# A hybrid decoder layer: 189 of TensorE's 128x128 transposes replaced by VectorE block transposes and on-chip transfers of 32x32 blocks

## Chip, cores and metric

The kernel runs on one core of a Trainium2 chip. The metric is device time in microseconds, the median of several executions; one more execution is taken with the hardware profiler, and its trace is what the views below read. Engines are called as in the profile: PE is TensorE's matmul side, PEld its weight loads, DVE is VectorE, ACT ScalarE, POOL GpSimd, SP SyncE, whose queue issues nearly all transfers.

## What is computed

One layer: a mixing part and a gated MLP, with RMSNorms. The mixing part, which the change touches, has an HGRN2 head group (4 heads) and a sliding-window attention group with sinks (8 query heads, 2 key heads). Cut to what matters:

```python
u = rmsnorm(x, norm_mix_w)                      # x: 2048 tokens x 1024
hq, hf, hi, hg, att = split(u @ w_in)
f = lb + (1 - lb) * sigmoid(hf);  k = 1 - f;  v = hi;  q = hq * 128 ** -0.5
# HGRN2: S_t = diag(f_t) S_{t-1} + k_t v_t^T,  o_t = S_t^T q_t   (4 heads of 128)
o_hg = rmsnorm(o, hg_norm_w) * silu(hg)
# attention: each block of 128 queries sees its own and the previous block of 128 keys
scores = q_att @ k_att.T / 8, masked to 0 <= distance < 128
p = exp(scores - m);  p = p / (sum(p) + exp(sink - m))
o_att = p @ v_att
h = x + concat(o_hg, o_att) @ w_out             # then the MLP with a causal convolution
```

The window is one block wide, so in a (query block, previous key block) pair exactly the keys above the diagonal are seen, and in the (query block, own key block) pair those on and below it. Scores of both fit in one 128x128 square: own key where key <= query, previous key elsewhere. The kernel keeps them so.

## The kernel before

Tokens are worked in two halves of 1024 (`NH` = 2, eight blocks of 128 in each). For each half come a mixing stage (tile pool `mix0`, `mix1`) and a feed-forward stage (`ffn0`, `ffn1`). Activations lie with features on partitions and tokens along the row; a "unit" is one projection to 128 features for 1024 tokens: 48 matmuls of 128x512, since each f32 operand is split in a high and a low part (`unit`, L218).

In the mixing stage:

- `att_keys` builds keys `KS` and values `V` (token-major, from four-to-a-bank transposes). The last block of keys and values of half 0 is kept in `kcarry` and `vcarry` (SBUF) for half 1.
- `attend(j)` is a generator for a pair of query heads j and j+4 (j = 0 to 3). Stage `qa` is the query unit. Stage `sc` makes, for each half-group g of 4 blocks, scores (L399), the maximum, exponentials (L421) and scaled probabilities `sc` (L426). Stages `pv` and `pw` (g = 0 and 1) transpose the probabilities with TensorE, four to a bank (`ppt`, L435), multiply them by two masks into `po` (own block) and `pp` (previous block) on DVE (L438), and multiply with `V` (`poT`, L446): own probabilities with the block's own values, previous ones with the previous block's.
- `hgrn(h)` is a generator for head h. Stages `f` and `q` are units; stage `l` builds the scores within a block over seven levels (L517 to L552) and leaves decayed keys `K`; stage `s` transposes `K` to `Kn` (`pkn`, L564, copied by ACT, L565) and forms the states `SS` (L571, L578); stage `p` forms the outputs (L590, L592), normalises them into `on` (L600), transposes them (`pot`, L605) and writes them to `hg` (L607 on ACT or L609 on DVE).
- `project_v` (`v0`, `v1`) are the values of two heads, `g` the gate units, `w` a gate's weights ahead of time, `m` the split of a finished output for the output projection.

The order of the stages is written out by hand in `ORDER`. It gives priorities: a planner then simulates all engines by its own costs and sets each engine's instruction order, so matmuls of a later unit stand in between those of an earlier stage. On the chip each engine and each queue keeps that order and waits by semaphores. Tiles of one `tag` share its `bufs` places: `sc` has 2, `pp` 4, `t4` (`ST`, `Kn`, `on`) 2, `SS` 1; weights have three places for raw data and two for their split parts. PSUM has four banks for units (`mm`) and two each for `hg` and `at`. `out_proj` follows with the mixed heads in the order 0, 4, 1, 5, 2, 6, 7, 3, so pair 3 and head 3 come last.

Of the kernel before, what the change touches and what calls it, by code (L numbers as in the profile page):

```python
# [17 lines left out]
P = 128  # L18
# [3 lines left out]
HALF = 1024  # L22
# [17 lines left out]
ORDER = ("f0 q0 l0 qa0 v0 s0 f1 p0 sc0 w0 pv0 q1 l1 qa1 pw0 g0 s1 qa2 sc1 w1 m4 f2 pv1 g1 p1 m1 q2 pw1 l2 "  # L40
         "sc2 v1 m0 pv2 qa3 s2 p2 pw2 f3 m6 q3 l3 m5 sc3 g2 pv3 pw3 m2 g3 s3 p3").split()
# [8 lines left out]
def hymba_layer(ctx: ExitStack, tc: tile.TileContext, a: dict, out: bass.AP, rows_out: bass.AP):  # L50
# [29 lines left out]
    ones = cp.tile([P, P], F32, name="ones")  # L80
    nc.vector.memset(ones, 1.0)
# [3 lines left out]
    nc.scalar.activation(warm, ones[:, 0:1], AF.Tanh)  # L85
# [5 lines left out]
    kc = cp.tile([P, 2, P], F32R, name="kcarry")  # L91
    vc = cp.tile([P, P], F32, name="vcarry")
# [6 lines left out]
    def constants():  # L99
# [3 lines left out]
        C.prevT = cp.tile([P, P], F32, name="prevT")  # L103
        for t, op, sgn in ((C.own, ALU.is_ge, 1), (C.ownT, ALU.is_ge, -1), (C.prevT, ALU.is_gt, 1)):
            nc.gpsimd.memset(t, 1.0)
            nc.gpsimd.affine_select(out=t, in_=t, compare_op=op, fill=0.0, base=0,
                                    pattern=[[-sgn, P]], channel_multiplier=sgn)
# [226 lines left out]

    def rows(kv):
        return slice(kv * HD, (kv + 1) * HD)

    def att_keys(hf, kv, invb, p):
# [6 lines left out]
        if hf:  # L345
            nc.vector.tensor_copy(KS[:, :, 0:P], kc)
            nc.vector.tensor_copy(V[:, 0], vc)
# [10 lines left out]
        for b in range(NB):  # L358
# [4 lines left out]
            nc.scalar.copy(V[:, 1 + 4 * b:5 + 4 * b].rearrange("p a b -> p (a b)"), pv)  # L363
        if hf + 1 < NH:
            nc.vector.tensor_copy(kc, KS[:, :, HALF:HALF + P])
            nc.vector.tensor_copy(vc, V[:, TT])
        return KS, V

    def attend(hf, j, X, invb, KS, V, mix, p):
# [9 lines left out]
        for g in range(NB):  # L379
# [46 lines left out]
            nc.vector.tensor_tensor(sc, sc, den.unsqueeze(3).to_broadcast([P, 2, 4, P]), op=ALU.mult)  # L426
            scs.append(sc)
        yield
        for g, sc in enumerate(scs):
            pm = []  # L430
            for kv in range(2):
                pm.append([p.tile([P, 4, P], F32, tag="pp", name=n, bufs=4) for n in ("po", "pp")])
                pt = ps("at", "ppt")
                for i in range(4):
                    nc.tensor.transpose(pt[:, i * P:(i + 1) * P], sc[:, kv, i], ident)  # L435
                ptv = pt.rearrange("p (i q) -> p i q", i=4)
                for dst, mk in zip(pm[kv], (C.ownT, C.prevT)):
# [764 lines left out]
```

## Time and profile before

| | |
|---|---|
| median of 3 runs | 2150.38 us (2150.18 to 2150.38) |
| the profiled execution: span, first to last instruction | 2149.0 us; no time beside the span is given, and the median stands 1.4 us above it |
| instructions | 29228 |
| PE busy | 2130.8 us (99%), 11271 matmuls |
| PEld busy | 1790.6 us (83%) |
| DVE busy | 1632.2 us (76%) |
| ACT busy | 1020.2 us (47%) |
| chain that ended last | PE 93%, DVE 5%, ACT 1% |
| DMA | 91147 packets, 254.41 MB, mean 118 GB/s |

A busy PE means that some matmul was under way: matmuls are pipelined, so the sum of their durations is more than the time they hold up what follows. A line of the groups view gives line, engine, operation, tile out<-in, shapes, count, then busy us and mean ns of one, then idle time of the engine just before and what ended it. A line of the timeline gives start and length in us, and "x8" means eight merged neighbours. The windows view is read in two stretches, 94 to 365 us for most of half 0's mixing and 1159 to 1441 us for that of half 1.

### The profile page before, as it was taken

How to read it: one execution, taken by the hardware profiler on the slowest of the kernel's cores; microseconds unless marked ns; L12 is line 12 of the kernel's file. 1: busy time of each engine (PE TensorE's matmuls, PEld its weight loads, DVE VectorE, ACT ScalarE, POOL GpSimd, SP SyncE). 2: the span in 40 equal slices, each digit the busy share in tenths (PEclk: the TensorE clock that was granted, in tenths of full speed). 3: DMA queues.
4: the chain of work that ended last, by engine and by line, in shares of the span. 5: the costliest groups of instructions: out<-in, count | busy, mean ns of one | idle time of the engine just before them, and what ended most of it. 6: DMA issues, size and time to landing. Idle time of an engine off the chain costs nothing.

```text
span 2149.0 us, 29228 instructions
## 1 busy us (share of the span) xinstructions
PE 2130.8 (99%) x11271; PEld 1790.6 (83%) x11271; DVE 1632.2 (76%) x2443; ACT 1020.2 (47%) x1818; POOL 16.2 (1%) x45
## 2 busy tenths in 40 slices
PE   8999999999999999999999999999999999999998
PEld 6988988888888888888889889888888888888887
DVE  6576768788887888785775767677988888787765
ACT  5445554564444445345634446535544444443453
POOL 2000000000000000000000000000000000000000
PEclk9999999999999999999999999999999999999999
DMA  4111012413332334974641111124223323359743
GB/s 158 40 30 40 31 30 79 137 62 125 94 122 89 103 118 147 371 255 145 217 138 40 30 31 33 40 75 158 69 104 103 118 84 122 95 187 398 236 147 133
DMA packets 91147, 254.41 MB, mean 118 GB/s; under 512 B 11136, under 2 KB 13952, under 8 KB 91008
## 3 DMA queue, kind: packets, MB, share of 16 engines
q1 hardware_dynamic: 90576, 252.29, 35.3%
q8 instruction: 88, 1.44, 0.3%
q14 instruction: 51, 0.42, 0.1%
q10 hardware_dynamic: 432, 0.27, 0.0%
HBM read 195.37 MB, written 57.15 MB: 118 GB/s over the span
## 4 chain that ended last, share of the span: by engine, by line
PE 93%; DVE 5%; ACT 1%; issue 1%; DMA 0%; SPq 0%; DVEq 0%; ACTq 0%
PE X L767 7%; PE X L766 7%; PE X L765 7%; PE pop L218 6%; PE q L218 4%; PE f L218 4%; PE hq L218 4%; PE Y L767 4%; PE Y L765 4%; PE Y L766 4%; PE pdx L954 3%; PE pdx L953 3%; PE pdx L952 3%; PE g L218 3%; PE pdy L953 3%; PE pdy L954 3%
## 5 line engine op out<-in xcount | busy, mean ns | idle before, releaser
L638 ACT CAST whi<-raw 128x1024 fp32r<-128x1024 f32 x88 | 92.7, 1053 | 115.5 <-PE X L766 71.1
L765 PE MATMUL X<-T,whi 128*128 128x512 f32 x352 | 136.9, 389 | 0.0
L766 PE MATMUL X<-T,whi 128*128 128x512 f32 x352 | 136.9, 389 | 0.0
L767 PE MATMUL X<-T,wlo 128*128 128x512 f32 x352 | 136.9, 389 | 0.0
L836 DVE SCALAR_TENSOR_TENSOR y<-ga,cw,y 128x1024 f32<-128x1024 f32 x88 | 112.7, 1280 | 25.9 <-ACT y L834 25.8
L639 DVE TENSOR_TENSOR wlo<-raw,whi 128x1024 fp32r<-128x1024 f32 x88 | 107.3, 1219 | 4.4 <-ACT whi L638 4.4
L771 ACT COPY u<-X 128x512 f32<-128x512 f32 x88 | 51.6, 586 | 122.5 <-PE X L767 122.2
L199 ACT CAST whi<-raw 128x1024 fp32r<-128x1024 f32 x58 | 60.5, 1048 | 98.8 <-issue 20.6
L639 DVE TENSOR_TENSOR xld<-raw,xhd 128x1024 fp32r<-128x1024 f32 x72 | 81.1, 1132 | 17.8 <-ACT xhd L638 17.6
L638 ACT CAST xhd<-raw 128x1024 fp32r<-128x1024 f32 x72 | 69.8, 978 | 39.1 <-DMA raw<-act0T 14.0
L218 PE MATMUL pop<-XL,whi 128*128 128x512 f32 x256 | 84.2, 392 | 0.9 <-DVE XL L230 0.9
L218 PE MATMUL pop<-XH,wlo 128*128 128x512 f32 x256 | 83.3, 391 | 0.8 <-DVE wlo L200 0.8
L218 PE MATMUL pop<-XH,whi 128*128 128x512 f32 x256 | 83.1, 396 | 0.8 <-ACT XH L229 0.5
L200 DVE TENSOR_TENSOR wlo<-raw,whi 128x1024 fp32r<-128x1024 f32 x58 | 70.5, 1220 | 9.8 <-ACT whi L199 9.8
L767 PEld LDWEIGHTS X<-T,wlo 128*128 128x128 f32 x352 | 66.1, 188 | 13.7
L766 PEld LDWEIGHTS X<-T,whi 128*128 128x128 f32 x352 | 66.1, 188 | 13.7
L765 PEld LDWEIGHTS X<-T,whi 128*128 128x128 f32 x352 | 66.0, 188 | 13.7
L630 PE MATMUL pvv<-whi,XH 128*128 128x256 f32 x256 | 73.0, 286 | 0.0
L631 PE MATMUL pvv<-whi,XL 128*128 128x256 f32 x256 | 72.9, 286 | 0.0
L632 PE MATMUL pvv<-wlo,XH 128*128 128x256 f32 x256 | 71.9, 285 | 0.0
L767 PE MATMUL X<-B,wlo 128*128 128x512 f32 x176 | 68.7, 390 | 0.7 <-DVE wlo L639 0.7
L765 PE MATMUL X<-T,Sh 128*128 128x512 f32 x176 | 68.7, 390 | 0.0
(390 smaller groups left out, 6399.2 us busy)
## 6 DMA issues: line engine op xcount, KB each, us to landing
wr<-in_w_down SPq DMA_DIRECT2D x90, 512.0 KB, 5.6
raw<-in_w_gate SPq DMA_DIRECT2D x44, 512.0 KB, 3.6
raw<-in_w_up SPq DMA_DIRECT2D x44, 512.0 KB, 3.6
raw<-act0T SPq DMA_DIRECT2D x20, 512.0 KB, 5.9
raw<-act1T SPq DMA_DIRECT2D x20, 512.0 KB, 5.6
act0B<-y SPq DMA_DIRECT2D x33, 256.0 KB, 2.3
act1B<-y SPq DMA_DIRECT2D x33, 256.0 KB, 2.4
raw<-in_w_out SPq DMA_DIRECT2D x16, 512.0 KB, 3.7
```

Source lines behind the costliest of these rows:

```text
L218: nc.tensor.matmul(o[b], w, x[:, bs], start=f, stop=l)
L630: nc.tensor.matmul(o[:, 0:256], xh[:, t], hi[:, c], start=kt == 0, stop=False)
L631: nc.tensor.matmul(o[:, 0:256], xl[:, t], hi[:, c], start=False, stop=False)
L632: nc.tensor.matmul(o[:, 0:256], xh[:, t], lo[:, c], start=False, stop=kt == KT - 1)
L638: nc.scalar.copy(h, src)
L639: return (eng or nc.vector).tensor_tensor(l, src, h.bitcast(F32), op=ALU.subtract)
L765: nc.tensor.matmul(o, wh[:, ws], xh, start=i == 0 and not more, stop=False, skip_group_check=more)
L766: nc.tensor.matmul(o, wh[:, ws], xl, start=False, stop=False, skip_group_check=more)
L767: nc.tensor.matmul(o, wl[:, ws], xh, start=False, stop=i == 3, skip_group_check=more)
L836: nc.vector.scalar_tensor_tensor(y, g[:, w:w + HALF], C.cw[:, ft, w:w + 1], y, op0=ALU.mult, op1=ALU.add)
L953: nc.tensor.matmul(o, wh[:, i, c], al[:, i, cols], start=False, stop=False, skip_group_check=more)
L954: nc.tensor.matmul(o, wl[:, i, c], ah[:, i, cols], start=False, stop=l, skip_group_check=more)
```

## The change

- Probabilities of pairs 0 to 2: DVE transposes each of the sixteen 32x32 blocks of a 128x128 square in place (`turned`), and 16 transfers on SP's queue put the blocks in their new places (`moved`). Pair 3 still goes through TensorE, and ACT then copies its transposed probabilities out of PSUM.
- Keys `Kn` and head outputs of heads 0 to 2: the same. Head 3 still goes through TensorE. The keys are turned at the end of stage `l`; the head outputs at the end of stage `p`, and what reads them is a new stage `x`.
- Values: `VD` is each block's values less the previous block's. Whole transposed probabilities times the previous values, plus own (masked) probabilities times `VD`, replaces the two masked products. The mask `prevT` goes; each probability tile is masked once in place of twice.
- The carried keys and values lie in DRAM and move by transfers. `ones` goes.
- `ORDER`: `q1` stands ahead of `pv0`, `q2` ahead of `m1`, and the four `x` stages are added. The last state is copied out earlier.

```diff
@@ -37,8 +37,8 @@
 UP_AFTER = 'T2'
-ORDER = ("f0 q0 l0 qa0 v0 s0 f1 p0 sc0 w0 pv0 q1 l1 qa1 pw0 g0 s1 qa2 sc1 w1 m4 f2 pv1 g1 p1 m1 q2 pw1 l2 "
-         "sc2 v1 m0 pv2 qa3 s2 p2 pw2 f3 m6 q3 l3 m5 sc3 g2 pv3 pw3 m2 g3 s3 p3").split()
+ORDER = ("f0 q0 l0 qa0 v0 s0 f1 p0 sc0 w0 q1 pv0 x0 l1 qa1 pw0 g0 s1 qa2 sc1 w1 m4 f2 pv1 g1 p1 q2 x1 m1 pw1 l2 "
+         "sc2 v1 m0 pv2 qa3 s2 p2 pw2 f3 m6 q3 x2 l3 m5 sc3 g2 pv3 pw3 m2 g3 s3 p3 x3").split()
 LEVELS = [1, 2, 4, 8, 16, 32, 64]
@@ -77,19 +77,18 @@
     nc.scalar.dma_start(nmw, a["norm_mix_w"])
-    ones = cp.tile([P, P], F32, name="ones")
-    nc.vector.memset(ones, 1.0)
     ident = cp.tile([P, P], F32, name="ident")
     warm = cp.tile([P, 32], F32, name="warm")[:, 0:1]
-    nc.scalar.activation(warm, ones[:, 0:1], AF.Tanh)
+    nc.vector.memset(warm, 1.0)
+    nc.scalar.activation(warm, warm, AF.Tanh)
     nc.gpsimd.memset(ident, 1.0)
     nc.vector.memset(halo, 0.0)
-    kc = cp.tile([P, 2, P], F32R, name="kcarry")
-    vc = cp.tile([P, P], F32, name="vcarry")
+    kc = dp.tile([P, 2, P], F32, name="kcarry")
+    vc = dp.tile([P, P], F32, name="vcarry")
@@ -100,8 +99,7 @@
         C.ownT = cp.tile([P, P], F32, name="ownT")
-        C.prevT = cp.tile([P, P], F32, name="prevT")
-        for t, op, sgn in ((C.own, ALU.is_ge, 1), (C.ownT, ALU.is_ge, -1), (C.prevT, ALU.is_gt, 1)):
+        for t, op, sgn in ((C.own, ALU.is_ge, 1), (C.ownT, ALU.is_ge, -1)):
             nc.gpsimd.memset(t, 1.0)
@@ -332,6 +330,17 @@
+    def moved(dst, src):
+
+        for a in range(4):
+            for c in range(4):
+                nc.sync.dma_start(dst[32 * c:32 * c + 32, :, 32 * a:32 * a + 32],
+                                  src[32 * a:32 * a + 32, :, 32 * c:32 * c + 32])
+
+    def turned(dst, src):
+
+        nc.vector.transpose(dst.rearrange("p a b -> p (a b)"), src.rearrange("p a b -> p (a b)"))
+
     def rows(kv):
@@ -343,8 +352,8 @@
         if hf:
-            nc.vector.tensor_copy(KS[:, :, 0:P], kc)
-            nc.vector.tensor_copy(V[:, 0], vc)
+            nc.sync.dma_start(KS.bitcast(F32)[:, :, 0:P], kc)
+            nc.sync.dma_start(V[:, 0], vc)
         kT, vT = [p.tile([P, HALF], F32, tag="f", name=n, bufs=2) for n in ("kT", "vT")]
@@ -361,12 +370,18 @@
             nc.scalar.copy(V[:, 1 + 4 * b:5 + 4 * b].rearrange("p a b -> p (a b)"), pv)
+        VD = p.tile([P, TT, P], F32, name="VD")
+        if hf:
+            nc.vector.tensor_tensor(VD, V[:, 1:], V[:, 0:TT], op=ALU.subtract)
+        else:
+            nc.scalar.copy(VD[:, 0], V[:, 1])
+            nc.vector.tensor_tensor(VD[:, 1:], V[:, 2:], V[:, 1:TT], op=ALU.subtract)
         if hf + 1 < NH:
-            nc.vector.tensor_copy(kc, KS[:, :, HALF:HALF + P])
-            nc.vector.tensor_copy(vc, V[:, TT])
-        return KS, V
-
-    def attend(hf, j, X, invb, KS, V, mix, p):
+            nc.sync.dma_start(kc, KS.bitcast(F32)[:, :, HALF:HALF + P])
+            nc.sync.dma_start(vc, V[:, TT])
+        return KS, V, VD
+
+    def attend(hf, j, X, invb, KS, V, VD, mix, p):
@@ -424,27 +439,38 @@
             nc.vector.tensor_tensor(sc, sc, den.unsqueeze(3).to_broadcast([P, 2, 4, P]), op=ALU.mult)
+            if j < ATT_J - 1:
+                pt = p.tile([P, 8, P], F32, tag="sc", name="pt", bufs=2)
+                for kv in range(2):
+                    t = p.tile([P, 4, P], F32, tag="pp", name="st", bufs=4)
+                    turned(t, sc[:, kv])
+                    moved(pt[:, 4 * kv:4 * kv + 4], t)
+                sc = pt
             scs.append(sc)
         for g, sc in enumerate(scs):
-            pm = []
+            whole, own = [], []
             for kv in range(2):
-                pm.append([p.tile([P, 4, P], F32, tag="pp", name=n, bufs=4) for n in ("po", "pp")])
-                pt = ps("at", "ppt")
-                for i in range(4):
-                    nc.tensor.transpose(pt[:, i * P:(i + 1) * P], sc[:, kv, i], ident)
-                ptv = pt.rearrange("p (i q) -> p i q", i=4)
-                for dst, mk in zip(pm[kv], (C.ownT, C.prevT)):
-                    nc.vector.tensor_tensor(dst, ptv, mk.unsqueeze(1).to_broadcast([P, 4, P]), op=ALU.mult)
+                own.append(p.tile([P, 4, P], F32, tag="pp", name="po", bufs=4))
+                if j < ATT_J - 1:
+                    whole.append(sc[:, 4 * kv:4 * kv + 4])
+                else:
+                    pt = ps("at", "ppt")
+                    for i in range(4):
+                        nc.tensor.transpose(pt[:, i * P:(i + 1) * P], sc[:, kv, i], ident)
+                    whole.append(p.tile([P, 4, P], F32, tag="pp", name="pw", bufs=4))
+                    nc.scalar.copy(whole[kv].rearrange("p i q -> p (i q)"), pt)
+                nc.vector.tensor_tensor(own[kv], whole[kv], C.ownT.unsqueeze(1).to_broadcast([P, 4, P]), op=ALU.mult)
             oT = ps("at", "poT")
                 noprev = hf == 0 and n == 0
-                for prev in (0,) if noprev else (1, 0):
+                for w in (1,) if noprev else (0, 1):
                     for kv in (1, 0):
                         r = rows(kv)
-                        nc.tensor.matmul(oT[r, i * P:(i + 1) * P], V[:, n + 1 - prev, r], pm[kv][prev][:, i],
-                                         start=noprev or prev == 1, stop=prev == 0)
+                        vv, pr = ((V, whole), (VD, own))[w]
+                        nc.tensor.matmul(oT[r, i * P:(i + 1) * P], vv[:, n, r], pr[kv][:, i],
+                                         start=noprev or w == 0, stop=w == 1)
             gs = slice(g * 512, (g + 1) * 512)
@@ -551,12 +577,16 @@
                                pl[s0:s0 + m, 0:TT * m].rearrange("p (c m) -> p c m", c=TT))
+        Kn = p.tile([P, TT, P], F32, tag="t4", name="Kn", bufs=2)
+        if h < HG - 1:
+            Kd = p.tile([P, TT, P], F32, tag="SS", name="Kd", bufs=1)
+            turned(Kd, K.rearrange("p (c t) -> p c t", t=P))
+            moved(Kn, Kd)
         yield
         kept = TT if hf + 1 < NH else TT - 1
-        Kn = p.tile([P, TT, P], F32, tag="t4", name="Kn", bufs=2)
-        for b in range(NB):
+        for b in range(NB if h == HG - 1 else 0):
             pk = ps("hg", "pkn")
@@ -599,10 +629,21 @@
                                     rs[:, 4 * b:4 * b + 4].unsqueeze(2).to_broadcast([P, 4, P]), op=ALU.mult)
+        if hf + 1 < NH:
+            nc.vector.tensor_copy(state[:, h], SS[:, TT - 1])
+        if h < HG - 1:
+            od = p.tile([P, TT, P], F32, tag="SS", name="od", bufs=1)
+            onT = p.tile([P, TT, P], F32, tag="t4", name="onT", bufs=2)
+            turned(od, on)
+            moved(onT, od)
+        yield
         for b, bs in halves():
-            pt = ps("hg", "pot")
-            for i in range(4):
-                nc.tensor.transpose(pt[:, i * P:(i + 1) * P], on[:, 4 * b + i], ident)
+            if h < HG - 1:
+                pt = onT[:, 4 * b:4 * b + 4].rearrange("p i t -> p (i t)")
+            else:
+                pt = ps("hg", "pot")
+                for i in range(4):
+                    nc.tensor.transpose(pt[:, i * P:(i + 1) * P], on[:, 4 * b + i], ident)
             if late:
@@ -612,8 +653,6 @@
                 nc.vector.tensor_tensor(lo[:, bs], g[:, bs], hi[:, bs].bitcast(F32), op=ALU.subtract)
-        if hf + 1 < NH:
-            nc.vector.tensor_copy(state[:, h], SS[:, TT - 1])
         yield
@@ -1104,15 +1143,15 @@
             p = pool(f"mix{hf}", stack=st, reuse_waits="tile")
-            KS, V = att_keys(hf, kv, invb, p)
+            KS, V, VD = att_keys(hf, kv, invb, p)
             mix = [None] * KT
             heads = [hgrn(hf, h, X, invb, vs, WG, gates, mix, p, None if h else f0) for h in range(HG)]
-            pairs = [attend(hf, h, X, invb, KS, V, mix, p) for h in range(HG)]
+            pairs = [attend(hf, h, X, invb, KS, V, VD, mix, p) for h in range(HG)]
             for name in ORDER:
                 stage, n = name[:-1], int(name[-1])
-                if stage in ("f", "q", "l", "s", "p"):
+                if stage in ("f", "q", "l", "s", "p", "x"):
                     next(heads[n])
```

## The prediction

> **What bounds the kernel.** I read the page first (busy shares, granted clock), then the two mixing stretches by window (94 to 365 us and 1159 to 1441 us, the only ones the change touches beyond a few constants), then TensorE's own list of waits, then the timeline around the transposes.
>
> ```profile
> span 2149.0 us, 29228 instructions
> PE 2130.8 (99%) x11271; PEld 1790.6 (83%) x11271; DVE 1632.2 (76%) x2443; ACT 1020.2 (47%) x1818; POOL 16.2 (1%) x45
> ```
> ```profile
> 94.00:365.00 271.00, 269.65 (x1911) 234.82 (x1911) 193.39 (x374) 135.46 (x368) 1.57 (x3) 1.00 0.15 46
> 1159.00:1441.00 282.00, 280.55 (x1993) 243.79 (x1992) 195.50 (x381) 140.63 (x386) 1.56 (x3) 1.00 0.15 45
> ```
> ```profile
> PE kv L218 <- ACT XH L232: 6.2, 2, 5.8
> ```
>
> The window rows give busy us of PE, weight loads, DVE, ACT and POOL, then the granted clock (1.00), the DMA share (0.15) and GB/s. TensorE is busy 269.65 of 271.00 us and 280.55 of 282.00 us; its largest wait of the whole run, 6.2 us in two times, is for the first x tiles at the start. So in these stretches time is TensorE's instruction stream. DVE is at 71% and ACT at 50% there, the DMA engines at 15%. What leaves TensorE's stream leaves the span, as long as nothing new stops it.
>
> **What goes: 189 transposes on TensorE.** The probabilities keep 32 of 128 (pair 3 alone), the keys 15 of 60, the head outputs 16 of 64 (head 3 alone). So 96 + 45 + 48 = 189 go.
>
> ```profile
> L435 PE MATMUL ppt<-ident,sc 128*128 128x128 f32 x128 | 18.0, 273 | 0.0
> L564 PE MATMUL pkn<-ident,K 128*128 128x128 f32 x60 | 8.2, 273 | 0.0
> L605 PE MATMUL pot<-ident,on 128*128 128x128 f32 x64 | 8.9, 272 | 0.0
> L435 PEld LDWEIGHTS ppt<-ident,sc 128*128 128x128 f32 x128 | 15.0, 140 | 1.7
> L564 PEld LDWEIGHTS pkn<-ident,K 128*128 128x128 f32 x60 | 6.9, 140 | 1.5 <-issue 0.8
> L605 PEld LDWEIGHTS pot<-ident,on 128*128 128x128 f32 x64 | 7.6, 140 | 0.9
> ```
> ```profile
> 97.92 1.03 PE L564 MATMUL pkn<-ident,K 128*128 128x128 f32 x8
> 98.72 0.31 PE L399 MATMUL psc<-KS,qh 128*128 128x128 f32 x1
> ...
> 129.63 0.60 PE L435 MATMUL ppt<-ident,sc 128*128 128x128 f32 x4
> 130.01 0.73 PE L218 MATMUL q<-XH,whi 128*128 128x512 f32 x2
> 130.58 0.62 PE L218 MATMUL q<-XL,whi 128*128 128x512 f32 x2
> 131.04 0.40 PE L218 MATMUL g<-XH,whi 128*128 128x512 f32 x1
> ...
> 140.59 1.03 PE L605 MATMUL pot<-ident,on 128*128 128x128 f32 x8
> 141.38 0.71 PE L218 MATMUL q<-XH,wlo 128*128 128x512 f32 x2
> 141.93 0.40 PE L218 MATMUL q<-XH,whi 128*128 128x512 f32 x1
> ```
>
> The busy column gives 18.0 x 96/128 + 8.2 x 45/60 + 8.9 x 48/64 = 26.3 us. But one transpose of 273 ns overlaps the next, and the last one's tail overlaps what follows, so I count from start to next start. Four of `ppt` start at 129.63, the next matmul at 130.01: 0.38 us. The pair behind them takes 0.57 us to the next start (130.01 to 130.58) where an undisturbed pair takes 0.46 (130.58 to 131.04), so entering and leaving a group costs another 0.11. 24 such groups go: 24 x 0.49 = 11.8 us. Eight of `pkn` take 0.80 us (97.92 to 98.72), 0.10 each: 45 x 0.10 = 4.5 us. Eight of `pot` take 0.79 and the pair behind 0.55: 0.88 for each of six heads, 5.3 us. Together 21.6 us; the busy sum is the upper end, 26.3, and the lower end is 189 x 0.095 (0.38/4), 18.0, with no price for a change of group. I take 21.6, since starts are what moves the stream.
>
> The Trainium skill ("Perfetto Trace Analysis", section Identifying the Most-Contended Engine) says that matmul occupancy misleads because matmuls are pipelined, and asks for weight-load time instead. By that rule the sum would be three quarters of 15.0 + 6.9 + 7.6, which is 22.1 us instead of 26.3; the starts in this trace agree with it.
>
> Nothing else of TensorE's changes in count: the attention products stay two for each block and head group, V_prev with the whole probabilities and the difference with the masked ones.
>
> **What is added to TensorE: waits.** A moved tile arrives by 16 transfers, so the first matmul that reads it may have to wait on up to 16 of them.
>
> ```profile
> L564 PEldq EVENT_SEMAPHORE  x14: 51/51/51, 95.8 to 1426.3; - x14
> ```
>
> Twelve probability groups and six key tiles are read so: 18 x (0 to 16) x 0.051 = 0 to 14.7 us. In the rows above nothing shows of such waits (the starts at 97.92 follow without a hole), because the sequencer runs ahead. I take 3 us, nearer to nothing, and keep both ends.
>
> **What is added elsewhere, and what covers it.** Each `moved` is 16 transfers on SP's queue: 24 for probabilities, 6 for keys, 6 for head outputs, 576 in all, 288 in a half.
>
> ```profile
> L198 SPq DMA_DIRECT2D raw<-in_w_f x8: 327/328/339, 19.1 to 1274.6; - x8
> rows<-sqr SPq DMA_DIRECT2D x8, 128.0 KB, 1.8
> q1 hardware_dynamic: 90576, 252.29, 35.3%
> q10 hardware_dynamic: 432, 0.27, 0.0%
> ```
>
> An issue takes 0.33 us, so SP gives 288 x 0.33 = 95 us of 271 to them; it waits most of that time now. The packets are of 128 B (8 or 16 to an engine and transfer). Their price isn't in the trace. Queue q1 gives 35.3% of 16 engines' span over 90576 packets, 134 ns for 2785 B, in proportion 6 ns for 128 B; q10's share rounds to 0.0%, so under 0.05% x 16 x 2149 / 432 = 40 ns for packets of 625 B. Between 6 and 40 ns a transfer of 8 packets ends in 0.05 to 0.32 us, within its issue. I take the issue as the limit: one `moved` is 16 x 0.33 + 1.8 to land = 7.1 us. For the 1024-wide tiles the upper end is 16 x 0.64 + 1.8 = 12.0.
>
> The probabilities of one half-group need two of them one behind the other, so from scaled probabilities to the first product: 0.6 + 32 x 0.33 + 1.8 = 13.0 us. What stands there now:
>
> ```profile
> 125.45 1.22 DVE L426 TENSOR_TENSOR sc<-sc,den 128x1024 f32<-128x1024 f32 x1
> 140.96 1.22 DVE L426 TENSOR_TENSOR sc<-sc,den 128x1024 f32<-128x1024 f32 x1
> 142.25 0.44 PE L446 MATMUL poT<-po,V 128*64 128x128 f32 x4
> 160.74 0.44 PE L446 MATMUL poT<-pp,V 128*64 128x128 f32 x4
> 162.63 0.73 PE L218 MATMUL q<-XH,wlo 128*128 128x512 f32 x2
> 174.55 0.22 PE L399 MATMUL psc<-KS,qh 128*128 128x128 f32 x1
> 271.96 1.22 DVE L426 TENSOR_TENSOR sc<-sc,den 128x1024 f32<-128x1024 f32 x1
> 282.57 0.44 PE L446 MATMUL poT<-pp,V 128*64 128x128 f32 x4
> 284.47 0.50 PE L218 MATMUL f<-XL,whi 128*128 128x512 f32 x1
> 303.24 0.22 PE L399 MATMUL psc<-KS,qh 128*128 128x128 f32 x1
> ```
>
> 126.7 to 142.25 is 15.6 us, 142.2 to 160.74 is 18.6, 273.2 to 282.57 is 9.4: the planner already lets q, g and f units of TensorE run between, and 13.0 lies among these. What grows is the attention chain as a whole: two `sc` buffers hold scores and moved probabilities, so the second half's scores now wait until the first half's are turned, some 3 us for a pair, 9 in a half. Between the last product of a pair and the first scores of the next there is room: 11.9 us from 162.63 to 174.55 (pairs 0 and 1) and 18.8 us from 284.47 to 303.24 (pairs 2 and 3), 30.7 in a half.
>
> Keys: 8.3 (1.2 + 7.1) to 13.2 us (1.2 + 12.0), used after a unit or a values stage. Head outputs go to ACT and DVE, not TensorE, with q1, q2 or q3 set between `p` and `x`. The carried keys and values go through DRAM, four transfers; their readers come tens of us later, so nothing. `ones`, `prevT` and their set-up: nothing.
>
> DVE pays and gains:
>
> ```profile
> L438 DVE TENSOR_TENSOR pp<-ppt,prevT 128x512 f32<-128x512 f32 x32 | 21.9, 684 | 0.0
> L475 DVE TENSOR_SCALAR K<-f 128x1024 f32<-128x1024 f32 x8 | 5.5, 692 | 0.2
> L200 DVE TENSOR_TENSOR wlo<-raw,whi 128x1024 fp32r<-128x1024 f32 x58 | 70.5, 1220 | 9.8 <-ACT whi L199 9.8
> L542 DVE COPY_PREDICATED ST<-lmask,plev 128x512 f32<-128x512 uint32 x15 | 14.4, 957 | 0.1
> L565 ACT COPY Kn<-pkn 128x512 f32<-128x512 f32 x12 | 6.6, 588 | 3.7 <-PE pkn L564 3.7
> ```
>
> No row shows a block transpose. Between 692 ns (1024 columns, one input) and 957 ns for 512 columns I take the 1220 ns row, an SBUF pass of 1024. In a half: 12 x 0.61 + 6 x 1.22 + 1.2 for the difference of values - 16 x 0.684 = +4.9 us (from -1.4 to +13.2). DVE then is busy 198 of 271 us, 207 at worst: off the path. ACT loses six copies of 0.588 us and gains four. Hidden.
>
> **The sum.** -21.6 + 3 = -18.6 us against the span of 2149.0: 2130.4. The median of the runs, 2150.38, stands 1.4 above the span; so 2131.8.
>
> **Rivals.**
>
> *The waits eat the gain.* The planner orders TensorE by its own costs; if it takes a `moved` for shorter than it is, TensorE reaches the product early and stands. 18 places x 1.2 us = 21.6 us is all of it: about 2150. For: 576 transfers of a shape the trace has none of. Against: it left 15.6 and 18.6 us where the data needed less.
>
> *Small transfers, on the other side.* SP's queue, or the engines behind it, needs longer than 0.33 us for a transfer of 128 B pieces. A pair has 64 in series, so at 0.66 us its chain grows by 21 us, three pairs by 63 us, less the 30.7 of room: 32 us in a half, 64 in both: 2150.4 - 21.6 + 64 = 2193. It decides from (30.7 + 10.8)/192 = 0.22 us more for each transfer (10.8 being half of 21.6), 0.55 in all. For: the 12.0 us upper end of a wide tile. Against: the 40 ns bound on a packet.
>
> The Trainium skill ("DMA: Bandwidth & Descriptors", section Rules for kernel authors) speaks for this one: it says that transfers under 64 KB pay mostly overhead and should be joined. These are of 16 and 32 KB. No transfer of that kind is in this trace; the nearest row, 128 KB in 1.8 us, neither confirms nor refutes it.
>
> *More than the sum.* All of 26.3 us goes and no wait shows: 2124.
>
> **How the numbers follow.** A measurement here tells 0.2% (4.3 us) from no change. My case 0.70, its own range 2124 to 2144 (26.3 without waits; 21.6 with all 14.7 of them); waits eat the gain 0.09, about 2150; small transfers, slower, 0.17, about 2193; more than the sum 0.04. So faster 0.74, same 0.09, slower 0.17. The range from 2122 to 2162 takes in the waits and the mild end of the small transfers.
>
> **What would show it.** Right: `ppt`, `pkn` and `pot` fall to 32, 15 and 16, TensorE stays at 99% in both stretches, its waits for moved tiles stay under 5 us, each stretch is some 9 us shorter, SP's issues stay at 0.33 us. Wrong: waits of TensorE for `pt` or `Kn`, holes before `poT`, issues longer than 0.55 us, a later pair-3 `psc`, weight loads late behind moved blocks on SP, or block transposes well over 1.9 us that make DVE late.

## The result, and the profile after

The changed kernel takes 2197.12 us (median of 4 runs), 2.2% more than before (2150.37 us in the same comparison; ratio 1.0219, 95% interval 1.0204 to 1.0233). Forecast were 2131.8 us and a range up to 2162. Page of the changed kernel, then its windows (columns as before: PE, PEld, DVE, ACT, POOL, granted clock, DMA share, GB/s):

```profile
span 2194.2 us, 29745 instructions
PE 2137.4 (97%) x11082; PEld 1793.8 (82%) x11082; DVE 1642.2 (75%) x2445; ACT 1019.9 (46%) x1815; POOL 19.5 (1%) x43
```
```profile
94.00:315.00 221.00, 217.79 (x1412) 187.90 (x1411) 147.22 (x276) 99.95 (x269) 1.04 (x2) 1.00 0.26 57
315.00:390.00 75.00, 56.47 (x408) 48.29 (x406) 51.08 (x106) 37.71 (x111) 0.52 (x1) 0.84 0.29 80
1159.00:1400.00 241.00, 238.91 (x1631) 208.56 (x1631) 154.48 (x281) 111.09 (x293) 1.04 (x2) 1.00 0.24 55
1400.00:1480.00 80.00, 60.36 (x451) 51.05 (x451) 53.26 (x109) 37.99 (x113) 0.52 (x1) 0.83 0.29 79
```

The same end of each mixing stage in the kernel before:

```profile
315.00:400.00 85.00, 83.14 (x538) 68.46 (x537) 64.49 (x114) 40.50 (x100) 0.00 (x0) 1.00 0.32 100
1400.00:1480.00 80.00, 78.06 (x473) 63.84 (x473) 58.73 (x104) 35.19 (x81) 0.00 (x0) 1.00 0.36 118
```

TensorE has 189 matmuls fewer, as forecast, yet its busy time rises by 6.6 us and it stands idle: adding up the holes between its matmuls gives 44.3 us, before 5.4. Of these, 38.2 us are in the last 75 to 80 us of each mixing stage. There it has too little to do, and the granted clock falls to 0.84 and 0.83, so that the matmuls that are left take longer. Up to 315 us (1400 us in the second half) it is nearly as full as before (217.79 of 221 us, 238.91 of 241).

What SP does, by the line of `moved`, from the answers on the transfers and on tile `pt`, and the queue's timeline:

```profile
L337 SPq DMA_DIRECT2D pt<-st x384: 585/599/1646, 122.4 to 1427.2; - x192
L337 SPq DMA_DIRECT2D Kn<-Kd x96: 585/609/1671, 94.7 to 1397.6; - x96
L337 SPq DMA_DIRECT2D onT<-od x96: 585/609/1767, 146.2 to 1438.1; - x96
DMA to landing us min/median/max: 1.8/1.8/3.9
...
  DVE po L463: 33.2, 11
```
```profile
122.41 22.17 SPq L337 DMA_DIRECT2D pt<-st  x32
144.68 0.53 SPq L196 DMA_DIRECT2D raw<-in_w_f  x1
146.19 10.97 SPq L337 DMA_DIRECT2D onT<-od  x16
157.27 21.02 SPq L337 DMA_DIRECT2D pt<-st  x32
```

An issue takes 0.60 us (min/median/max in ns), not 0.33, and from one start to the next it is 0.64 us in the median. The 32 transfers of a group hold SP 22 us; the second group, transposed at 150 us, waits until 157 for the outputs ahead of it. DVE in the same stretch:

```profile
121.67 1.31 DVE L342 STREAM_TRANSPOSE st<-sc 128x512 f32<-128x512 f32 x2
...
150.04 1.29 DVE L342 STREAM_TRANSPOSE st<-sc 128x512 f32<-128x512 f32 x2
151.26 1.25 DVE L463 TENSOR_TENSOR po<-pt,ownT 128x512 f32<-128x512 f32 x2
...
170.08 0.68 DVE L463 TENSOR_TENSOR po<-pt,ownT 128x512 f32<-128x512 f32 x1
...
179.84 0.70 DVE L463 TENSOR_TENSOR po<-pt,ownT 128x512 f32<-128x512 f32 x1
180.44 0.68 DVE L403 TENSOR_TENSOR ql<-att,qh 64x512 fp32r<-64x512 f32 x1
```

The first group's probabilities are masked (`po`) 29.6 us behind their transposes, the second's 20 and 29 us. Two things hold these masks. The transfers do for most: over both halves, 14 of the 24 masks start within 1 us of the landing of their last block, and the mean distance from landing to mask is 4.2 us. The rest is DVE's written order: the first group's blocks had landed at 135.5 and 145.8 us, and its masks stand behind the second group's transposes, at 151.3 us and later. Only after the second group's masks comes `ql`, the first step of the next pair's scores. So the lateness adds up: the scores of pairs 1, 2 and 3 start at 186.3, 261.2 and 343.5 us where they started at 174.5, 233.3 and 303.2. The fourth pair starts 40 us late, and the holes lie there: by then TensorE has little else left to do.

### The profile page after: what moved, and what is told of

Same layout as the page of the kernel before. It is cut to its first block, busy times and chain, and to the rows that moved or that the text cites. A ratio compares the mean times of both kernels' runs of the same rounds, so it can differ in the third digit from the quotient of the medians.

```text
span 2194.2 us, 29745 instructions
## 1 busy us (share of the span) xinstructions
PE 2137.4 (97%) x11082; PEld 1793.8 (82%) x11082; DVE 1642.2 (75%) x2445; ACT 1019.9 (46%) x1815; POOL 19.5 (1%) x43
## 2 busy tenths in 40 slices
DMA packets 199505, 267.47 MB, mean 122 GB/s; under 512 B 118720, under 2 KB 122304, under 8 KB 199360
## 4 chain that ended last, share of the span: by engine, by line
PE 89%; SPq 4%; DVE 4%; ACT 2%; issue 1%; DMA 1%; ACTq 0%; DVEq 0%
PE X L806 7%; PE X L805 7%; PE X L804 7%; PE pop L216 6%; SPq L337 4%; PE f L216 4%; PE hq L216 4%; PE q L216 4%; PE Y L804 4%; PE Y L806 4%; PE Y L805 4%; PE pdx L993 3%; PE pdx L991 3%; PE pdx L992 3%; PE g L216 3%; PE pdy L993 3%
## 5 line engine op out<-in xcount | busy, mean ns | idle before, releaser
L678 DVE TENSOR_TENSOR xld<-raw,xhd 128x1024 fp32r<-128x1024 f32 x72 | 81.0, 1131 | 19.9 <-ACT xhd L677 19.6
L677 ACT CAST xhd<-raw 128x1024 fp32r<-128x1024 f32 x72 | 69.6, 978 | 40.6 <-DMA raw<-act0T 12.5
L804 PE MATMUL Z<-B,whi 128*128 128x512 f32 x176 | 68.7, 390 | 0.0
```

Source lines behind the costliest of these rows:

```text
L677: nc.scalar.copy(h, src)
L678: return (eng or nc.vector).tensor_tensor(l, src, h.bitcast(F32), op=ALU.subtract)
L804: nc.tensor.matmul(o, wh[:, ws], xh, start=i == 0 and not more, stop=False, skip_group_check=more)
```

## The experiments

All are timed against the kernel before on the same chip. "st to po" is the mean from the start of a block transpose to the start of the mask that reads its probabilities, over 24 tiles; "pair 3" is the start of its first value matmul in half 0; "holes" are the gaps between TensorE's matmuls.

| kernel | median us | ratio, 95% interval | st to po, us | pair 3, us | holes, us |
|---|---|---|---|---|---|
| before | 2150.2 | | | 347.3 | 5.4 |
| changed | 2197.1 | 1.0204 to 1.0233 | 25.2 | 378.3 | 44.3 |
| nomove: no transfers | 2138.6 | 0.9928 to 0.9961 | 1.7 | 339.4 | 9.0 |
| vdonly: nothing moved | 2158.7 | 1.0026 to 1.0054 | | 347.2 | 8.7 |
| hgonly: keys, outputs moved | 2147.5 | 0.9977 to 0.9996 | | 342.4 | 7.0 |
| ptonly: probabilities moved | 2163.0 | 1.0046 to 1.0076 | 23.4 | 363.2 | 20.3 |
| flat: long rows | 2197.2 | 1.0203 to 1.0234 | | | |
| poolhalf: POOL issues half | 2185.8 | 1.0151 to 1.0182 | 22.6 | 373.3 | 36.4 |
| serial: late, little issued | 2182.4 | 1.0133 to 1.0164 | 26.0 | 374.5 | 40.2 |
| bounce: by DRAM | 2153.5 | 1.0005 to 1.0024 | 19.4 | 348.2 | 19.3 |
| bouncehp: with priority | 2149.5 | 0.9987 to 1.0005 | 18.8 | 340.8 | 15.2 |

The time goes more with the start of pair 3 and with the holes than with "st to po": ptonly has 23.4 us there and poolhalf 22.6, but poolhalf takes 22.8 us longer.

### Are the transfers the loss? (nomove, vdonly, hgonly, ptonly)

nomove:

```diff
-                    t = p.tile([P, 4, P], F32, tag="pp", name="st", bufs=4)
-                    turned(t, sc[:, kv])
-                    moved(pt[:, 4 * kv:4 * kv + 4], t)
+                    turned(pt[:, 4 * kv:4 * kv + 4], sc[:, kv])
```
(keys and outputs likewise.)

> No block transfers: the readers take the block-transposed tiles as they stand. Left out of the computation: the movement of the 32x32 blocks between the partition quarters, so attention and head outputs are mixed up. VectorE transposes, V_prev and the difference, the new order and the removed TensorE transposes stay. Theory 'SyncE's queue': all of the loss comes from the 576 transfers, which occupy SP at 0.60 us each; without them the predicted saving of 21.6 us shows, 2126 to 2137 us, granted clock 0.99 to 1.00, PE idle under 20 us. Rival 'order and buffers': the new order (x steps, q1 and m1 moved) and the two sc buffers starve TensorE whoever moves the blocks: 2165 us or more, with PE idle in 315 to 390 us as now. Rival 'VectorE': the transposes and the difference put VectorE on the path: above 2150 us.

2138.6 us, 1.6 above the range of its theory: without the transfers the kernel is faster than before, and the mask follows its transpose at once.

```profile
124.57 1.31 DVE L342 STREAM_TRANSPOSE pt<-sc 128x512 f32<-128x512 f32 x2
125.80 1.25 DVE L461 TENSOR_TENSOR po<-pt,ownT 128x512 f32<-128x512 f32 x2
```

58.5 us hang on the transfers; order and VectorE's transposes can't make up the loss. (The tiles `st`, `Kd` and `od`, which the transfers read, go with them, so buffers are not told apart here.) The gain of 11.7 us is short of the 18.6 forecast, so something else costs. The next three put the TensorE transposes back, all or in part (`if j < 0` for `if j < ATT_J - 1`, `if h < 0` for `if h < HG - 1`).

> V_prev and the difference, the x steps and the new order stay; all probabilities, keys and head outputs are transposed on TensorE again, and no block is moved. Theory 'TensorE's saving is real, order and difference cost something': the kernel without transfers stood at 2138.6 us, and its transposes took 19.2 us less of TensorE than before's (ppt 12.7 to 3.3, pkn 7.0 to 1.6, pot 6.0 to 1.6 us, start to start); putting them back gives 2155 to 2158 us. Rival 'VectorE's block transposes ate the rest': order and difference are free, so 2149 to 2151 us.

> Only keys and head outputs go by VectorE and block transfers: 96 transfers a half in place of 288; the probabilities are transposed on TensorE. Theory 'SyncE's queue, with a threshold': 96 issues of 0.60 us hold SP 58 us of the 280 us of a mix stage, too little to make the attention chain late, so only the 9.8 us of TensorE show: 2141 to 2149 us. Rival 'each transfer costs alike' (0.10 us, 58.6 us over 576 transfers): 192 transfers cost 19.5 us and give 2158 to 2168 us.

> Only probabilities go by VectorE and block transfers: 192 a half; keys and head outputs are transposed on TensorE. Theory 'SyncE's queue, the attention chain': the 16 transfers a half-group stay a serial step of 9.6 us twice in each group, before the probabilities are read, so most of the loss stays: 2175 to 2192 us. Rival 'each transfer costs alike': 384 transfers cost 39 us beside 9.8 us of transposes put back: 2185 to 2190 us. Rival 'keys and outputs do the damage': under 2160 us.

vdonly stands at 2158.7 us, 0.7 above the range of its theory: `VD`, the order and the `x` steps cost 8.4 us together, with holes of 8.7 us and small delays spread over many lines. (vdonly sends the probabilities of all four pairs through ACT's copy, the change only those of pair 3, so the 8.4 us are near what the change pays, not a measurement of it.) vdonly less nomove, 20.1 us, is what the 189 transposes are worth (forecast 21.6). hgonly then gains 11.2 us on vdonly, where the transposes that it saves took 9.8 us in the kernel before, from start to start: 192 transfers of 0.61 us cost nothing here. ptonly, at 2163.0 us below what its theory gave, loses 4.4 us on vdonly although it saves TensorE some 9.4 (`ppt` from start to start, 12.7 before, 3.3 in nomove). So 192 transfers cost nothing, 384 cost about 14 and 576 cost 58.5 us: there is no one price for each. Since the 192 and the 384 move different tiles, these runs don't tell the number from the place in the chain. Keys and outputs, harmless alone, add to it where probabilities move too.

### What makes an issue long? (flat, micro)

flat: VectorE transposes one column quarter at a time, so that a block row of a tile lies in one piece.

```diff
-nc.sync.dma_start(dst[32*c:32*c+32, :, 32*a:32*a+32], src[32*a:32*a+32, :, 32*c:32*c+32])
+nc.sync.dma_start(dst[32*c:32*c+32, a].rearrange("p i r -> p (i r)"),
+                  src[32*a:32*a+32, c].rearrange("p i r -> p (i r)"))
```
(one transfer of probabilities or outputs; the 96 transfers of keys keep their form.)

> The 480 transfers of probabilities and outputs become two-dimensional: VectorE writes each column quarter's blocks side by side (four transposes in place of one), so that a transfer moves 32 rows of 512 or 1024 contiguous bytes. [...] Theory 'SyncE's queue, by the pattern': the issue takes 0.60 us because of the third dimension, as 0.33 us of the two-dimensional weight loads suggests; then 0.33 us here, a half's transfers hold SP 108 us in place of 173, and the time is 2130 to 2150 us. Rival 'SyncE's queue, whatever the pattern': the issue stays at 0.58 to 0.62 us and the time at 2188 to 2200 us. Rival 'packets': fewer and longer packets (118720 under 512 B becomes about 25000) bring the time down although the issue does not change.

2197.2 us, as the change, and the issue stays at 0.59 us. The packets under 512 B fall from 118720 to 44992 and the time doesn't follow, so packets don't look like the price. VectorE has 174 instructions and 11.5 us of work more here, which could hide a small gain; bounce, below, is the cleaner test. (Probabilities and outputs lie in another order of blocks here, and what is computed from them is not the layer's; the transfers are as many as in the change.)

> No part of the layer is computed: series of transfers of one form each on SP (and one each on the queues of ACT and POOL), with nothing to wait for, and after them bursts of 100 matmuls of 128x512 with gaps of growing length between. Theory 'pattern': two-dimensional forms issue in about 0.33 us, also within SBUF, three-dimensional ones in 0.60 us or more, whichever their bytes. Rival 'place': every transfer from SBUF to SBUF, or from a quarter of the partitions, takes 0.60 us. Rival 'wait': the 0.60 us are a wait for the DMA side to take descriptors, so the first transfers of a series are quick and later ones slow. Clock: after a gap of TensorE under about 2 us the granted clock stays 1.00; after one above some bound between 2 and 10 us it is 0.5 for a few us, as in the tail of the changed kernel's mix stage.

Answers on the lines of this kernel: 128 rows of 512 B (`wide`), 32 rows of 512 B (`row`), then 32 rows of 4, 8 and 1 pieces of 128 B (L78, L82, L86; L78 is the form of the change), 128 rows of 4 pieces (`all`), then from DRAM 128 rows of 8 pieces (`fromdram`), the reads of bounce below (`turn`) and rows of 512 B (`dramrow`), the same rows to DRAM, and the form of the change on the other two queues.

```profile
L69 SPq DMA_DIRECT2D wide<-src x8: 465/586/811, 2.4 to 7.6; - x8
L74 SPq DMA_DIRECT2D row<-src x16: 508/588/716, 8.3 to 18.2; - x16
L78 SPq DMA_DIRECT2D blk<-src x16: 598/600/677, 18.8 to 28.6; - x16
L82 SPq DMA_DIRECT2D blk<-src x16: 599/608/1453, 29.2 to 39.0; - x16
L86 SPq DMA_DIRECT2D blk<-src x16: 575/589/607, 40.5 to 50.0; - x16
L89 SPq DMA_DIRECT2D all<-src x4: 639/640/686, 50.6 to 52.7; - x4
L92 SPq DMA_DIRECT2D fromdram<-way x4: 560/664/780, 53.8 to 56.0; - x4
L95 SPq DMA_DIRECT2D turn<-way x4: 682/780/1282, 56.7 to 59.6; - x4
L99 SPq DMA_DIRECT2D dramrow<-way x8: 430/430/745, 60.4 to 64.0; - x8
L102 SPq DMA_DIRECT2D todram<-src x8: 430/430/431, 64.5 to 67.8; - x8
L106 ACTq DMA_DIRECT2D actblk<-src x16: 592/613/957, 2.0 to 12.8; - x16
L110 POOL DMA_DIRECT2D poolblk<-src x16: 548/548/661, 2.2 to 10.5; - x16
```

Of the three theories none holds alone. Issued one behind the other from SBUF to SBUF, the forms take 0.59 to 0.64 us, one run of bytes in a row or eight, which speaks against "pattern" and for "place", and rows of 512 B with DRAM at one end take 0.43. But with DRAM at one end the pattern counts: 8 pieces in a row take 0.66 us, bounce's reads 0.78. And part of it is "wait", for rows: at the head of a series flat's rows take 0.51 to 0.52 us and those behind 0.59, and serial's 128 rows of 512 B, each waiting for the one before, take 0.46 to 0.47 where `wide` takes 0.59. The form of the change takes 0.59 us at the head of a series and 0.60 behind. So 0.60 us is its price, and why it is that and not 0.33 stays open between the ends and the form. From SP, ACT and POOL that form takes 0.60, 0.61 and 0.55 us.

### Load, or lateness? (ghost, serial, bounce, poolhalf)

ghost is the kernel before with the change's transfers added, into a tile `idle` that nobody reads (`ghost(sc[:, kv])`, `ghost(K)`, `ghost(on)`).

> The kernel before, whole, with 576 more transfers of the change's form (32 partitions, 4 runs of 128 bytes), issued on SP when probabilities, keys and outputs are ready, into a tile that nobody reads: the load on SP and on the DMA engines without anybody waiting. Theory 'a longer chain': the load alone costs little, 2150 to 2160 us. Rival 'SP blocked': weights and other transfers queue behind 173 us of issues a half, and the time is 2175 us or more. Rival 'packets and DMA engines': likewise 2175 us or more.

2253.3 us (1.0463 to 1.0498), as both rivals gave. It still tells nothing apart, since the transfers read `sc`, and the next scores wait for that buffer: TensorE waits 47.2 us in 8 times for `psc` by way of DVE's `sc`. The load was not without a waiter.

serial is nomove with a chain of whole copies in place of the 16 transfers:

```diff
+                    nc.sync.dma_start(pt[:, 4 * kv:4 * kv + 4], t)
+                    for _ in range(HOPS[kv]):
+                        nc.sync.dma_start(t[:, 0], pt[:, 4 * kv])
+                        nc.sync.dma_start(pt[:, 4 * kv], t[:, 0])
```

> The kernel without transfers (readers take the block-transposed tiles; blocks are not moved between quarters), but each of the 48 probability tiles of the three pairs goes through a chain of whole-tile copies, one after another: 1 copy and 2 or 4 round trips of a 512 byte slice, 14 transfers a group in place of 32, each waiting for the one before. Some 11 us of delay for the first tile and 20 us for the second, about what the 16 and 32 issues of 0.60 us make, while SP is held about 7 us a group. Keys and outputs are not delayed. Theory 'a longer chain': most of the loss comes back without the load, 2160 to 2190 us (the kernel with only probabilities moved stood 24 us above the one with neither: 2163.0 less 9.4 of transposes put back, against 2138.6, is 15). Rival 'SP blocked': 2138 to 2150 us.

(`HOPS` is 2 and 4. There are 24 such tiles, not 48, so 168 transfers.) 2182.4 us: 43.8 of the 58.5 us come back with under a third of the transfers, at 0.46 to 0.52 us an issue, some 40 us of SP in a half. The mask comes 26.0 us behind its transpose, as in the change, and pair 3 comes at 374.5 us. Lateness is enough; the number of issues isn't needed. SP's queue is not free in serial, since it also stands 127 us in both halves until copies have landed, so "SP blocked" would have to show as late weights. In one mixing stage TensorE's weight loads wait at most 2.1 us for split weights in serial, 0.9 in the change and 1.9 in the kernel before; ACT waits 4.2 us for raw weights in the change, in both stages, and not at all in serial. Weights stuck behind the blocks are not the loss.

bounce writes the transposed tile to DRAM whole and reads it back in four:

```diff
+        for u, src in enumerate(srcs):
+            nc.sync.dma_start(d[:, u * k:u * k + k], src)
+        for c in range(4):
+            nc.sync.dma_start(dst[32 * c:32 * c + 32].rearrange("p i (a r) -> p i a r", r=32),
+                              d[:, :, 32 * c:32 * c + 32].rearrange("(a p) i r -> p i a r", a=4))
```

> The same blocks go by way of DRAM: the transposed tile is written there whole and read back in four transfers, one for each partition quarter, both halves of the heads of a probability tile in one read: 6 transfers in place of 32 for each group of probabilities, 5 in place of 16 for keys and outputs; 66 issues a half in place of 288. The 128 byte packets stay and more bytes move. Theory 'SyncE's queue': SP holds 40 to 60 us a half in place of 173, the chain of a pair falls by some 15 us, 2128 to 2150 us, although a block lands twice. Rival 'packets and DMA engines': as many short packets, so 2185 us or more. Rival 'order and buffers': 2165 us or more.

2153.5 us, 3.5 above its theory's range and below its rivals'. 197005 packets against the change's 199505, and 12.5 MB more, but 43.6 us less: neither packets nor bytes are the cause. The reads issue in 0.68 us, the writes in 0.33, 66 of both in a half.

> All 576 transfers as in the change, but those that read the odd column quarters are issued by POOL, which does little else, so SP issues 144 a half (86 us) and POOL 144. Same bytes, packets and transfers. Theory 'serial issue on one queue': the 16 transfers of a tile take 4.8 us in place of 9.6 us, the chain of a pair grows by about half as much, 2150 to 2172 us. Rival 'packets and DMA engines': nothing changes, 2190 us or more. Rival 'order and buffers': 2190 us or more as well.

2185.8 us, in no theory's range: only 11.3 us come back where 25 to 47 were expected. Timelines of SP, POOL and DVE in that kernel:

```profile
124.70 11.09 SPq L337 DMA_DIRECT2D pt<-st  x16
125.08 8.87 POOL L337 DMA_DIRECT2D pt<-st  x16 [25.20 <-DVE st L342]
...
150.90 1.29 DVE L342 STREAM_TRANSPOSE st<-sc 128x512 f32<-128x512 f32 x2
152.12 1.25 DVE L463 TENSOR_TENSOR po<-pt,ownT 128x512 f32<-128x512 f32 x2
```

The first group's transfers are issued by 135.8 us, half the time as hoped, but DVE masks them at 152.1, behind the second group's transposes: that is where the planner wrote the mask. DVE waits only 2.1 us in all for moved probabilities, in the change 33.2, and a mask starts 11.9 us behind the landing of its last block in the mean, in the change 4.2. Here the written order holds the chain.

### Buffers, or order? (two, three, pp6, bouncepp6, afterhp, bouncehp)

`ql` follows `po` at once in the change, and `st`, `po`, `qh`, `ql` share four buffers. To make room for more, `VD` is given up: `whole -= own` in place on DVE, weights `V[:, n]` and `V[:, n + 1]`.

> The changed kernel with all its 576 transfers, but without the tile of differences: the own part is subtracted from the transposed probabilities in place (one more VectorE operation of 0.68 us for each probability tile), and V[n] and V[n+1] are the weights as before. It is the control for the next three, which need the 4 KB a partition that the difference took. All theories: 2190 to 2215 us.

> The control with a third buffer for scores and moved probabilities (sc). Theory 'sc buffers': the next pair's scores no longer wait for the pair before; 20 us or more below the control. Theory 'pp buffers' or 'length of the chain': within 8 us of the control.

> The control with six in place of four buffers for transposed tiles, masked probabilities and split queries (pp). Theory 'pp buffers': st holds its buffer until the transfers have read it, so the next pair's qh and ql wait for them; with two more, 20 us or more below the control, and ql of the second pair starts some 10 us earlier. Theory 'sc buffers' or 'length of the chain': within 8 us of the control.

> The way by DRAM (66 issues a half) with the control's values and six pp buffers. Theory 'pp buffers': 2138 to 2147 us, under before. Theory 'length of the chain alone': 2150 to 2158 us, as the way by DRAM with four buffers (2153.5 us).

two 2215.5, three 2215.1, pp6 2207.4, bouncepp6 2162.8 us. two lies just above what was expected, and bouncepp6 above both its ranges, 9.3 us over bounce. A third `sc` buffer gives nothing and two more `pp` buffers 8.1 us of 65; `ql` of the second pair starts at 180 to 182 us in the first three. Neither pool of buffers is the main cause. (The single place of `SS`, which `Kd` and `od` also take, was not varied.) two takes 18 us more than the change: its subtraction runs 32 times at 0.68 us, 21.8 us of DVE, and the two of `VD`, 2.3 us, go. So nearly all of what DVE has more to do comes back in the time, though DVE is busy only three quarters of the time.

The next two give the attention's steps a higher priority:

```diff
+OFF, FIRST = 200, ("sc", "pv", "pw")
...
-                    next(pairs[n])
+                    with tc.high_priority(OFF) if stage in FIRST else ExitStack():
+                        next(pairs[n])
```

> The changed kernel, same operations, transfers, buffers and list of steps; only the attention's score and value steps are given a higher priority where the order on each engine is worked out, so that VectorE and TensorE come to the moved probabilities earlier: the fourth pair's first value matmul stands some 100 matmuls earlier on TensorE, the fourth head's 60 later. Theory 'written order': 2160 to 2180 us, 15 us or more below the change. Theory 'length of the transfer, 0.60 us an issue one after another': the readers then wait for the transfers instead, 2185 to 2205 us.

> The way by DRAM (66 issues a half, 2153.5 us) with the same higher priority of the attention steps. Theory 'written order': the first group's probabilities are read some 25 us earlier than 39 us behind their transposes, and the time falls to 2138 to 2148 us, below the kernel before. Theory 'length of the transfer': 2150 to 2158 us, as without.

afterhp takes 2200.4 us (1.0217 to 1.0248): with the transfers as they are, this other order gains nothing. (What it waits for instead is not shown.) bouncehp takes 2149.5, 4.0 under bounce, between the ranges of its two theories: where the transfers are short, the order is worth at most a little, since the intervals touch. So in the change the length of the transfers holds most of the chain, as the 14 masks behind a landing say; once they are shorter, as in poolhalf, the written order holds it. The two together for poolhalf weren't tried.

### A version that beats both? (keysA, keysB)

hgonly is the best of those that compute the layer. Since `VD` seemed to cost 8.4 us, keysA takes hgonly with the attention of before, keysB also before's order with the `x` steps put in.

> As the kernel with only keys and outputs moved (192 transfers, 2147.5 us), but with the attention of before: two masks, V[n] and V[n+1], no difference. The new order stays. Theory 'the difference costs': the 8.4 us by which the kernel with neither transfer stands above before come mostly from V_prev and the difference (a copy of the transposed probabilities before the mask, on ACT, ahead of VectorE), so 2139 to 2143 us. Rival 'the order costs': 2146 to 2148 us.

> As the run before it, with the order of before and only the x steps put in (pv0 ahead of q1 again, x0 behind q1). Theory 'the difference costs': as the run before it, within 3 us. Rival 'the order costs': 2138 to 2142 us, 5 us or more below the run before it. By either, if keys and outputs cost nothing beyond their TensorE transposes (the measured 11.2 us), this kernel stands at about 2139 us, 0.5% under before.

2160.0 and 2159.5 us (1.0032 to 1.0062 and 1.0031 to 1.0061): both theories miss. Which of the two orders is taken makes no difference, and with two masks per tile on VectorE the moved keys and outputs do cost, 12.5 us against hgonly, with holes of 19.6 us, the larger ones late in the stage. Why the difference of values costs without moved tiles and pays with them, these runs don't settle. The best remains hgonly, 2147.5 us, under both kernels, but by 0.13% (0.04 to 0.23).

## Why the prediction was wrong, by its own steps

- **"An issue takes 0.33 us": the step that failed.** It was taken from weight loads out of DRAM; in the form of the change, 32 rows of four pieces between two SBUF tiles, it is 0.60, in micro and in the kernels. One `moved` is then 16 x 0.60 + 1.8 = 11.4 us by the prediction's own sum, not 7.1, and a half gives 173 us of SP to them, not 95. With the room between issues it is more: 16 in a row hold SP 10.2 to 11.9 us, and a half some 193 us. The 1.8 us to land were right. The bound on packets, put against this rival, spoke of the DMA engines, and the limit was the queue that issues (flat: 62% fewer short packets, the same time).
- **"Lies among these".** 13.0 us for a half-group was set against 15.6 and 18.6 us that the kernel before had between scaled probabilities and product, as if those were spare; the third row beside them, 9.4 us, was shorter than 13.0 already. nomove shows that they weren't: where the data come earlier, the mask follows in 1.7 us, pair 3 starts 8 us sooner and the gain shows. Serial shows the other side: 26 us of delay, 43.8 us lost.
- **The rival "small transfers"** gave 2193 for 0.66 us and decided from 0.55; measured were 0.60 and 2197.1. Its mechanism, 64 transfers of a pair in series and the room between pairs, is what the trace shows: 40 us later in a half for pair 3, where it had 32. That its time comes so near is partly luck: its formula gives 2171 us for the 0.60 us of an issue and 2198 for the 0.67 us that starts lie apart in the mean, and in both it leaves out the lower clock and the 8.4 us below. It had 0.17, for want of a row of a transfer within SBUF: I took the queue's largest group of equal rows, and those differed in ends and in form. The Trainium skill's rule that the prediction set beside it ("DMA: Bandwidth & Descriptors", section Rules for kernel authors: join small transfers) agrees with bounce, whose 128 to 512 KB transfers take 43.6 us off; bounce also goes by DRAM, so the size is not the only difference.
- **189 transposes, 21.6 us:** 20.1 (vdonly less nomove); from start to start the traces of before and nomove give 19.2. Right.
- **"Nothing" for values, order and `x` steps:** some 8.4 us (vdonly). Wrong, and it alone would have taken 40% of the 21.6 us.
- **VectorE:** `STREAM_TRANSPOSE` took 0.68 us (forecast 0.61) and 1.24 (1.22), VectorE in all 10.0 us more (9.8). Keys and outputs hidden: right in hgonly.
- **Waits of TensorE for moved tiles:** 7.1 us for `pt` in three times, against 3 taken. Most of the loss doesn't show there but as holes before whatever is next in TensorE's order (the heads' outputs 8.2 us, `pdiag` 7.2, `plev` 4.5, `psc` 3.2): a wait's line names the last link, not the chain. "Weight loads late behind moved blocks", the prediction's other sign, did not come: in a mixing stage TensorE's weight loads wait at most 0.9 us for split weights, before 1.9.

The sum against before's span: -20.1 for the transposes and +38.9 for holes (44.3 - 5.4) leave 26.4 of the 45.2 us. The trace's record of the granted clock has it at 0.50 for 51.2 us of the two mixing stages, 7.9 of them holes; at half the pace the other 43.3 us do the work of 21.6. So the lower clock is an estimated 21.6 us, and 4.8 are left for small terms.

## What to carry to other kernels

Price an issue by a row with the same two ends (SBUF to SBUF, or DRAM at one) and the same form, not by the biggest group of rows in the trace; where there is no such row, as here, measure one first. Multiply it by the longest series that one reader waits for. Work taken off a full engine is a gain only while the chain that feeds its last stretch stays short: look at what runs when the filler has run out. When many small transfers rearrange one tile, few large ones with a stop in DRAM can be quicker, though every block lands twice (66 issues a half against 288, 43.6 us less).

## What the hardware showed beside

Short holes can cost twice, by the clock that follows them. In micro, bursts of 100 matmuls follow gaps of growing length; windows of it:

```profile
90.00:100.00 10.00, 8.67 (x39) 6.87 (x38) 1.12 (x3) 0.00 (x0) 0.00 (x0) 1.00 0.01 2
120.00:130.00 10.00, 7.68 (x27) 5.86 (x26) 2.03 (x5) 0.00 (x0) 0.00 (x0) 0.83 0.00 0
240.00:250.00 10.00, 5.04 (x12) 4.01 (x13) 4.51 (x10) 0.00 (x0) 0.00 (x0) 0.50 0.00 0
```

After a gap of 1.3 us (first row) the granted clock stays 1.00; after 2.3 us (second row) and after every longer one up to 24 us (the third row has 8.3) it is 0.5 for 3.3 to 5.7 us of the burst behind, and then full again. The changed kernel's last stretches, with holes of up to 3.6 us, run at 0.83 to 0.84 for the same reason: eight times there the clock falls to 0.5, for 3.4 to 10.2 us. But the length of one hole doesn't decide. In the change a hole of 3.1 us, ending at 228.8 us, leaves the clock at 1.00, and it falls at 373.9 us behind holes of 0.7 and 0.5 us. The clock's own record may say why: in both traces it falls only at whole multiples of 3.41 us from the first fall, so the same hole can lie well or badly to these steps. The Trainium skill ("TensorE: Matmul & The Clock Gate", section HAM oscillation) warns of idle gaps above about 3.4 us; in micro 2.3 us did it, both times that it was tried.
